# A SwiGLU feed-forward stage whose additions move from GpSimd to VectorE, one per step

## The chip, the core and the metric

The kernel runs on one core of one Trainium2 chip. The metric is the device time of one execution in microseconds. The engines are named as in the profile: PE (TensorE matmuls), DVE (VectorE), ACT (ScalarE), POOL (GpSimd) and SP (SyncE, which here only issues DMAs). A DMA goes to the queue of the engine that issues it; each engine works through its own instructions strictly in order.

## The reference

One block of a streaming encoder: RMSNorm, an input projection, two attention mixers, an output projection with a residual, then the feed-forward part, which is all that the change touches. Everything is float32, S = 2048, D = 1024, D_FF = 2816:

```
h2 = rmsnorm(x, norm2_g)
g = einsum('bsd,df->bsf', h2, w_gate)
u = einsum('bsd,df->bsf', h2, w_up)
x = x + einsum('bsf,fd->bsd', silu(g) * u, w_down)
return rmsnorm(x, normf_g)
```

## The kernel before

**Blocks.** Every product of the feed-forward part is done as a 2x2 product of blocks by a scheme with seven products (P1 to P7) in place of eight; its price is sums of blocks ahead of the products and of results behind them. Each factor is split into a rounded high part (a CAST on ACT, L930) and the rest (a subtraction on DVE, L931), and each product of blocks is three matmuls per 128 rows of the contraction: high by high, high by low, low by high. A step is one of the seven products.

**Stages.** The tokens come in two halves of 1024. In each half there are 11 pairs of a gate and an up matrix, each of a gate's and an up's 14 steps (ORDER: P1, P2, P6, P5, P7, P3, P4) of 12 matmuls (L1054 to L1056); then the Down stage, 7 products of 11 steps of 12 matmuls (L1163 to L1165). Half 0's Down also prepares the other half's h2 blocks (next_h2). In half 0, down_sums makes the four sums of w_down's blocks and writes them to DRAM (wd_d), once for both halves.

**Banks and results.** A matrix has three PSUM banks: A takes P1, P6, P7 and P4, C takes P2, B takes P5 and P3. After P1, P6 and P7, ACT copies A to a tile `u` (L1064); after P7, DVE adds B to it (L1066) and the block (1,1) is done. P3 then accumulates on in B, so its first matmul waits for L1066; P2's and P3's results are added at L1069 and L1072. A gate's block goes through Silu on ACT (L1083), an up's is multiplied with the gate's: block (0,0) on POOL, the other three on DVE (L1087). After the last of the four, `activations` makes the block sums of the result (three on POOL, one on DVE) and POOL's queue writes all seven blocks to DRAM (a_d, L1096).

**What sets the order.** The text of the loop over `steps` (L1257) issues, for step `at`: loads up to 12 steps ahead (6 in Down) on SP, all four sums of a weight matrix when its P1 is 6 steps ahead (L1018 to L1021, POOL), splits 4 steps ahead (3 in Down), the step's matmuls, and what follows from its result. down_sums comes behind the gate's P5: its two loads, four sums on DVE (the same lines L1018 to L1021) and four writes on SP (L1119). `late` holds squares and final scalings of a Down stage, one per step. Weight tiles share 6 buffers (`raw`), split operands 7, and all tiles of [128, 512] float32 (sums, `u`, `t`, x, squares) one pool of 18; a tile's buffer is handed on when its last reader is done.

Of the kernel before, what the change touches and what calls it, by code (L numbers as in the profile page):

```python
# [19 lines left out]
P = 128  # L20
# [39 lines left out]
def block_kernel(  # L60
# [848 lines left out]
    with ExitStack() as c4:  # L909
        def pool(name, bufs):  # L910
            return c4.enter_context(tc.tile_pool(name=name, bufs=bufs, reuse_waits="tile"))

        hop, rawp, opp, t2p, np_ = pool("hop", 1), pool("rawF", 6), pool("opF", 7), pool("t2", 18), pool("nf", 1)
        psF = c4.enter_context(tc.tile_pool(name="psF", bufs=8, space=PSUM, reuse_waits="tile"))
# [7 lines left out]

        def t2(name):
            return t2p.tile([P, 512], F32, name=name, tag="t2")

# [54 lines left out]
        def next_h2(half):  # L980

            for q in range(2):
                cs = slice(q * 256, (q + 1) * 256)
                for k0 in (0, 2):
                    ks_ = slice(k0, k0 + 2)

                    def put(p, src):
                        hi, lo = ops_h[p]
                        split(hi[:, ks_, cs], lo[:, ks_, cs], src)

                    b = {}
# [11 lines left out]
                    nc.gpsimd.tensor_tensor(b12, b22, b12, ALU.subtract)  # L1003
# [5 lines left out]
                    nc.gpsimd.tensor_tensor(b11, b22, b11, ALU.subtract)  # L1009
                    nc.gpsimd.tensor_tensor(b21, b21, b11, ALU.subtract)  # L1010
                    yield
                    put("P6", b11)
                    put("P4", b21)
                    yield

        def sums(a11, a12, a21, a22, eng):
            s = {p: t2(f"s{p}") for p in ("P5", "P6", "P7", "P3")}
            eng(s["P5"], a21, a22, ALU.add)  # L1018
            eng(s["P6"], s["P5"], a11, ALU.subtract)
            eng(s["P7"], a11, a21, ALU.subtract)  # L1020
            eng(s["P3"], a12, s["P6"], ALU.subtract)  # L1021
            return dict(s, P1=a11, P2=a12, P4=a22)

        late = []

        class Matrix:
# [10 lines left out]
            def sum(self):  # L1037
                r = self.r
                self.s = sums(r[0][:, 0], r[0][:, 1], r[1][:, 0], r[1][:, 1], nc.gpsimd.tensor_tensor)

# [37 lines left out]
            def done(self, i, j):  # L1078

                d = self.dst  # L1080
                if not self.up:
                    o = t2("u") if (i, j) == (1, 0) else d[i, j]
# [8 lines left out]
            def activations(self):  # L1091
# [6 lines left out]
                t1, t2_, t4 = t2("t"), t2("t"), t2("t")  # L1098
                sub = nc.gpsimd.tensor_tensor
                put("P1", b11)  # L1100
                put("P3", b22)
                put("P2", b21)
                sub(t1, b12, b11, ALU.subtract)
                sub(b12, b22, b12, ALU.subtract)
                put("P5", t1)
                put("P7", b12)
                sub(t2_, b22, t1, ALU.subtract)
                put("P6", t2_)
                nc.vector.tensor_sub(t4, b21, t2_)
                put("P4", t4)  # L1110

        def down_sums(n):
            r = []
            for f in (n, n + NF // 2):
                r.append(raw([P, 2, 512], "wd"))
                nc.sync.dma_start(out=r[-1].rearrange("p a b -> p (a b)"), in_=w_down[f * P:(f + 1) * P, :])
            s = sums(r[0][:, 0], r[1][:, 0], r[0][:, 1], r[1][:, 1], nc.vector.tensor_tensor)
            for p in ("P5", "P6", "P7", "P3"):
                nc.sync.dma_start(out=wd_d[PLACE[p], n // 2, :, n % 2, :], in_=s[p])  # L1119

        class Down:
# [50 lines left out]
            def square(self, t, i):  # L1172
                sq = t2("sq")
                ss = small.tile([P, 1], F32, name="ssf", bufs=20)
# [13 lines left out]
            def take(self, p):  # L1188
# [17 lines left out]
                elif p == "P4":  # L1206
                    self.add(p, 1, 0)
                    late.extend(partial(self.square, b, 1) for b in q)
                    late.extend(partial(self.finish, b) for b in q)


        steps = []
        for half in range(2):
# [6 lines left out]
            for p in ORDER:  # L1220
                steps += [("down", dn, p, n) for n in range(NF // 2)]
        loads, summed, made = [0], [0], [0]

        def advance_loads(at):
# [32 lines left out]
        for at, s in enumerate(steps):  # L1257
            down = s[0] == "down"
            advance_loads(at)
            advance_sums(at + 6)  # L1260
            advance_splits(at + (3 if down else 4))
            if down:
                s[1].multiply(s[2], s[3])
                if s[2] == "P1" and s[3] < 8:
                    s[1].load_x(s[3])
                if s[1].half == 0:
# [72 lines left out]
```

## Time and profile before

| | |
|---|---|
| median of 3 runs | 2978.04 us (2973.07 to 2979.21) |
| the profiled execution | 2973.52 us, its span 2971.7 us |
| granted TensorE clock, mean | 0.978 of full speed |
| busy in the span | PE 95%, DVE 58%, ACT 46%, POOL 34% |
| the feed-forward part | from about 1562 us of the span to its end |
| half 0: gate and up / Down | 1562 to 2090 / 2090 to 2310 us |
| half 1: gate and up / Down | 2310 to 2750 / 2750 to 2971.7 us |

Times are counted from the span's start. Matmuls overlap in the rows: each is listed with the time from its start to its modelled end, so the pace is read from one start to the next. Behind an instruction, square brackets hold the idle time of its engine before it and what ended that. The clock is the share of full speed granted to TensorE; its two levels are 2.4 and 1.2 GHz. A few matmuls have no record in the trace.

### The profile page before, as it was taken

What the parts mean: (1) busy time and instruction counts of PE and PEld (TensorE: products, weight loads), DVE (VectorE), ACT (ScalarE), POOL (GpSimd) and SP (SyncE); (2) the same over time, 40 slices, a digit from 0 to 9 for tenths busy, and PEclk for the clock granted to TensorE, in tenths of its full rate; (3) what the DMA queues carried; (4) which work ended last, traced back from release to release, by engine and by line L of the source; (5) the groups of instructions that cost most, each with busy time, mean ns of one, the idle gap of its engine ahead of it and who ended that gap; (6) DMA issues with size and microseconds to landing.
All of it is one profiled execution on the core that took longest, in us unless ns stands there. A gap on an engine that the chain in (4) does not pass through costs nothing.

```text
span 2971.7 us, 40975 instructions
## 1 busy us (share of the span) xinstructions
PE 2825.7 (95%) x14538; PEld 2355.2 (79%) x14538; DVE 1715.2 (58%) x3213; ACT 1354.9 (46%) x2752; POOL 1016.4 (34%) x1313
## 2 busy tenths in 40 slices
PE   8999999999999999999997898888999999999997
PEld 7889888789998888777875676777788788888886
DVE  5321411198889888873227656656686655555555
ACT  5211111287788788873334232223455333333443
POOL 3210631134443433331113545534221555554001
PEclk9999999999999999999997999999999999999999
DMA  5342533533532333215444434344767323223764
GB/s 194 125 138 93 150 110 117 181 85 105 145 102 63 97 103 105 82 56 202 163 149 159 145 125 135 118 133 142 252 213 235 122 101 105 103 92 107 259 202 159
DMA packets 160701, 406.75 MB, mean 137 GB/s; under 512 B 24128, under 2 KB 40656, under 8 KB 160496
## 3 DMA queue, kind: packets, MB, share of 16 engines
q1 hardware_dynamic: 121520, 292.31, 31.4%
q0 software_dynamic: 38944, 111.82, 10.6%
q8 instruction: 114, 1.87, 0.3%
q14 instruction: 91, 0.75, 0.1%
q10 hardware_dynamic: 32, 0.01, 0.0%
HBM read 272.35 MB, written 131.66 MB: 136 GB/s over the span
## 4 chain that ended last, share of the span: by engine, by line
PE 73%; DVE 8%; POOL 7%; issue 5%; ACT 4%; DMA 2%; DVEq 0%; POOLq 0%; SPq 0%; ACTq 0%
PE psF L1054 6%; PE psM L255 6%; PE psM L253 6%; PE psM L254 6%; PE psF L1055 6%; PE psF L1056 6%; PE ps L707 6%; PE psS L550 4%; PE psS L551 3%; PE psF L1164 3%; PE psF L1165 3%; PE psF L1163 3%; PE psO L642 3%; DVE wop L931 3%; PE psO L636 2%
## 5 line engine op out<-in xcount | busy, mean ns | idle before, releaser
L1054 PE MATMUL psF<-hhP,wop 128*128 128x512 f32 x1232 | 492.3, 405 | 83.1 <-DVE u L1066 64.4
L1055 PE MATMUL psF<-hlP,wop 128*128 128x512 f32 x1232 | 492.3, 400 | 5.6 <-DVE hlP L931 5.6
L1056 PE MATMUL psF<-hhP,wop 128*128 128x512 f32 x1232 | 490.2, 398 | 1.7 <-DVE wop L931 1.7
L1054 PEld LDWEIGHTS psF<-hhP,wop 128*128 128x128 f32 x1232 | 239.2, 194 | 155.9 <-DVE u L1066 77.8
L580 ACT ACTIVATE p_sb<-p_sb,mx 128x1024 f32<-128x1024 f32 (+7 forms) x384 | 343.8, 902 | 25.1 <-DVE mx L561 17.6
L1055 PEld LDWEIGHTS psF<-hlP,wop 128*128 128x128 f32 x1232 | 239.3, 194 | 53.9 <-DVE hlP L931 6.9
L1056 PEld LDWEIGHTS psF<-hhP,wop 128*128 128x128 f32 x1232 | 238.6, 194 | 53.9 <-DVE wop L931 2.6
L550 PE MATMUL psS<-ks,q 128*128 128x512 f32 (+2 forms) x640 | 271.3, 424 | 3.8 <-DVE mx L567 3.5
L707 PE MATMUL ps<-ident,p_sb 128*128 128x128 f32 x1632 | 251.1, 274 | 9.3 <-ACT thd L733 5.3
L1164 PE MATMUL psF<-dop 128*128 128x512 f32 x616 | 240.2, 390 | 2.7 <-DVE dop L931 2.7
L1163 PE MATMUL psF<-dop 128*128 128x512 f32 x616 | 239.9, 389 | 0.2 <-ACT dop L930 0.2
L1165 PE MATMUL psF<-dop 128*128 128x512 f32 x616 | 239.7, 389 | 0.0
L931 DVE TENSOR_TENSOR wop<-sP,wop 128x512 fp32r<-128x512 f32 x176 | 176.1, 1012 | 98.3 <-ACT wop L930 97.4
L551 PE MATMUL psS<-ks,q 128*128 128x512 f32 (+2 forms) x640 | 232.8, 364 | 0.0
L707 PEld LDWEIGHTS ps<-ident,p_sb 128*128 128x128 f32 x1632 | 194.6, 141 | 40.5 <-ACT thd L733 7.5
L930 ACT CAST wop<-sP 128x512 fp32r<-128x512 f32 x176 | 107.2, 622 | 218.8 <-PE psF L1056 108.5
L253 PE MATMUL psM<-hTh,whi 128*128 128x512 f32 (+1 forms) x528 | 205.7, 391 | 0.5 <-ACT hTh L220 0.5
L254 PE MATMUL psM<-hTl,whi 128*128 128x512 f32 (+1 forms) x528 | 205.5, 390 | 0.6 <-DVE hTl L221 0.5
L255 PE MATMUL psM<-hTh,wlo 128*128 128x512 f32 (+1 forms) x528 | 205.1, 389 | 0.0
L931 DVE TENSOR_TENSOR dop<-wr,dop 128x512 fp32r<-128x512 f32 x154 | 112.4, 730 | 134.4 <-ACT dop L930 134.1
L931 DVE TENSOR_TENSOR wop<-wr,wop 128x512 fp32r<-128x512 f32 x132 | 148.2, 1125 | 64.9 <-ACT wop L930 64.6
L930 ACT CAST dop<-wr 128x512 fp32r<-128x512 f32 x154 | 95.8, 622 | 184.2 <-PE psF L1165 165.9
(210 smaller groups left out, 6338.8 us busy)
## 6 DMA issues: line engine op xcount, KB each, us to landing
ar<-a_d SPq DMA_DIRECT2D x70, 512.0 KB, 3.5
wr<-in_w_gate_dram SPq DMA_DIRECT2D x44, 512.0 KB, 3.9
wr<-in_w_up_dram SPq DMA_DIRECT2D x44, 512.0 KB, 4.4
a_d<-u POOLq DMA_DIRECT2D x88, 256.0 KB, 3.2
wr<-wd_d SPq DMA_DIRECT2D x40, 512.0 KB, 4.4
a_d<-t POOLq DMA_DIRECT2D x66, 256.0 KB, 3.2
q<-fq_d SPq DMA_DIRECT2D x64, 256.0 KB, 3.9
q<-dq_d SPq DMA_DIRECT2D x64, 256.0 KB, 3.9
```

What stands on the lines that cost most here:

```text
L253: nc.tensor.matmul(ps, lh, rh, start=k == 0, stop=False)
L254: nc.tensor.matmul(ps, lh, rl, start=False, stop=False)
L255: nc.tensor.matmul(ps, ll, rh, start=False, stop=k == DK - 1)
L550: nc.tensor.matmul(pm[:, 0:mw], q[:, m, 0, qc], ks[:, m, cols], start=True, stop=False)
L580: nc.scalar.activation(pv, pv, AF.Exp, scale=-1.0, bias=st[m], accum_out=acc)
L707: nc.tensor.transpose(ps[:, (2 * i + s) * P:(2 * i + s + 1) * P], p_of(u, s, m, k0 + i), ident)
L931: nc.vector.tensor_sub(lo, src, f32(hi))
L1054: nc.tensor.matmul(acc, o[:, 0, ks_], hh[:, k, :], start=first and k == 0, stop=False, **go)
L1055: nc.tensor.matmul(acc, o[:, 0, ks_], hl[:, k, :], start=False, stop=False, **go)
L1056: nc.tensor.matmul(acc, o[:, 1, ks_], hh[:, k, :], start=False, stop=k == 3, **go)
L1163: nc.tensor.matmul(acc, a[:, 0, bs], w[:, 0, :], start=first and n == 0, stop=False, **go)
L1164: nc.tensor.matmul(acc, a[:, 0, bs], w[:, 1, :], start=False, stop=False, **go)
```

## The change

All sums of weight blocks (`sums`), the product of block (0,0), the block sums of the result and the subtractions of next_h2 are done by DVE; POOL keeps the DMA issues and the small operations of the final norm. `sums` becomes a generator: one sum is made per call, when the matrix's P1, P2, P6 and P5 come into the window of 7 steps ahead (6 before). down_sums becomes one too: its loads are issued at the gate's P2 and one sum each at P6, P5, P7 and P3, and the writes go out on POOL's queue instead of SP's. `activations` is called twice, after the blocks (0,1) and (1,0). The pool of 18 buffers becomes four rings: `s` (5, sums of gate and up weights), `g` (6, gate blocks), `u` (3, up blocks), `t` (3, sums of the result and of w_down), and one buffer for squares. Loads go out 11 steps ahead instead of 12; Down's x loads start one step later and take the rings' buffers; at the end of Down, squares and final scalings alternate.

```diff
-        hop, rawp, opp, t2p, np_ = pool("hop", 1), pool("rawF", 6), pool("opF", 7), pool("t2", 18), pool("nf", 1)
+        hop, rawp, opp, np_ = pool("hop", 1), pool("rawF", 6), pool("opF", 7), pool("nf", 1)
+        RINGS = dict(s=5, g=6, u=3, t=3)
+        rings = {r: pool(f"ring_{r}", n) for r, n in RINGS.items()}
...
-                    nc.gpsimd.tensor_tensor(b11, b12, b11, ALU.subtract)
+                    nc.vector.tensor_sub(b11, b12, b11)
...
-        def sums(a11, a12, a21, a22, eng):
-            s = {p: t2(f"s{p}") for p in ("P5", "P6", "P7", "P3")}
-            eng(s["P5"], a21, a22, ALU.add)
...
+        def sums(a11, a12, a21, a22, ring):
+            def put(p, a, b, op):
+                o = t2(ring, f"s{p}")
+                nc.vector.tensor_tensor(o, a, b, op)
+                return o
+            s5 = put("P5", a21, a22, ALU.add)
+            yield "P5", s5
+            s6 = put("P6", s5, a11, ALU.subtract)
+            yield "P6", s6
+            yield "P7", put("P7", a11, a21, ALU.subtract)
+            yield "P3", put("P3", a12, s6, ALU.subtract)
...
-                self.s = sums(r[0][:, 0], r[0][:, 1], r[1][:, 0], r[1][:, 1], nc.gpsimd.tensor_tensor)
+                if not hasattr(self, "s"):
+                    r = self.r
+                    b = r[0][:, 0], r[0][:, 1], r[1][:, 0], r[1][:, 1]
+                    self.s, self.rest = dict(P1=b[0], P2=b[1], P4=b[3]), sums(*b, "s")
+                self.s.update([next(self.rest)])
...
-                    d[i] = t2("u")
+                    d[i] = t2("u" if self.up else "g", "u")
...
-                    (nc.gpsimd if (i, j) == (0, 0) else nc.vector).tensor_mul(g, g, d[i, j])
-                    if (i, j) == (1, 0):
-                        self.activations()
+                    nc.vector.tensor_mul(g, g, d[i, j])
+                    if (i, j) in ((0, 1), (1, 0)):
+                        self.activations((i, j) == (1, 0))
...
+                if last:
+                    put("P2", b21)
+                    sub(self.t2, b21, self.t2)
+                    put("P4", self.t2)
+                    return
+                t1, self.t2 = t2("t", "t"), t2("t", "t")
                 put("P1", b11)
+                sub(t1, b12, b11)
+                put("P5", t1)
+                sub(self.t2, b22, t1)
+                sub(b12, b22, b12)
+                put("P7", b12)
                 put("P3", b22)
+                put("P6", self.t2)
...
-            s = sums(r[0][:, 0], r[1][:, 0], r[0][:, 1], r[1][:, 1], nc.vector.tensor_tensor)
-            for p in ("P5", "P6", "P7", "P3"):
-                nc.sync.dma_start(out=wd_d[PLACE[p], n // 2, :, n % 2, :], in_=s[p])
+            yield
+            for p, o in sums(r[0][:, 0], r[1][:, 0], r[0][:, 1], r[1][:, 1], "t"):
+                nc.gpsimd.dma_start(out=wd_d[PLACE[p], n // 2, :, n % 2, :], in_=o)
+                yield
...
-                    self.xs[t, i] = t2("x1")
+                    self.xs[t, i] = t2("ggtttuuusssssggg"[2 * t + i], "x1")
...
-                if loads[0] >= at + (12 if s[0] == "in" else 6):
+                if loads[0] >= at + (11 if s[0] == "in" else 6):
...
-                if s[0] == "in" and s[2] == "P1":
+                if s[0] == "in" and s[2] in SUM_AT:
                     s[1].sum()
...
-            advance_sums(at + 6)
+            advance_sums(at + 7)
...
-                if s[1].half == 0 and not s[1].up and s[2] == "P5":
-                    down_sums(s[1].n)
+                if s[1].half == 0 and not s[1].up:
+                    if s[2] == "P2":
+                        wd = down_sums(s[1].n)
+                    if s[2] != "P1":
+                        next(wd, None)
```

In the order that follows, the number at a row's start is its place on the engine; `wd` is a tile of w_down, `wr` one of a gate's or up's weights, `psF` a PSUM bank, `wop` a split operand, and the numbers behind names tell tiles apart. DVE before, in half 0, from the gate's P2 add (L1069) to behind its P7 add (L1066):

```order
2366 L1069 TENSOR_TENSOR u_18452<-psF_18457,u_18452 128x512
2367 L931 TENSOR_TENSOR wop_18552<-wr_18350,wop_18552 128x512
2368 L1018 TENSOR_TENSOR sP5_18521<-wd_18517,wd_18519 128x512
2369 L1019 TENSOR_TENSOR sP6_18522<-sP5_18521,wd_18517 128x512
2370 L1020 TENSOR_TENSOR sP7_18523<-wd_18517 128x512
2371 L1021 TENSOR_TENSOR sP3_18524<-wd_18519,sP6_18522 128x512
2372 L931 TENSOR_TENSOR wop_18569<-sP6_18473,wop_18569 128x512
2373 L931 TENSOR_TENSOR wop_18586<-sP5_18472,wop_18586 128x512
2374 L1066 TENSOR_TENSOR u_18548<-psF_18504,u_18548 128x512
```

DVE after the change at the same place (P2 add L1081, P7 add L1078; L934 is the split, L1023 a sum, L1113 the last block sum of the result):

```order
2434 L934 TENSOR_TENSOR wop_18531<-wr_18369,wop_18531 128x512
2435 L1081 TENSOR_TENSOR u_18456<-psF_18463,u_18456 128x512
2436 L1113 TENSOR_TENSOR t_18412<-u_18292,t_18412 128x512
2437 L934 TENSOR_TENSOR wop_18553<-wr_18369,wop_18553 128x512
2438 L1023 TENSOR_TENSOR sP7_18550<-wd_18478 128x512
2439 L1023 TENSOR_TENSOR sP5_18608<-wr_18526 128x512
2440 L934 TENSOR_TENSOR wop_18573<-sP6_18482,wop_18573 128x512
2441 L1023 TENSOR_TENSOR sP3_18570<-wd_18480,sP6_18522 128x512
2442 L1023 TENSOR_TENSOR sP6_18628<-sP5_18608,wr_18525 128x512
2443 L934 TENSOR_TENSOR wop_18590<-sP5_18458,wop_18590 128x512
2444 L1023 TENSOR_TENSOR sP7_18647<-wr_18525,wr_18526 128x512
2445 L1078 TENSOR_TENSOR u_18546<-psF_18509,u_18546 128x512
```

The four sums of w_down no longer stand in one piece ahead of the gate's P7 add: two of them, with the last block sum of the result, stand behind the P2 add, each with a split or a sum of the next matrix's weights beside it, and three sums of that matrix (sP5, sP6, sP7 from `wr`) have come in from POOL.

POOL before, behind the products of a pair of half 0 (DMAs L1096 write the result's blocks, L1104 and L1107 are block sums, the rest sums of weights):

```order
816 L1096 DMA a_d_99<-u_18287 128x512
817 L1096 DMA a_d_99<-t_18422 128x512
818 L1096 DMA a_d_99<-u_18198 128x512
819 L1107 TENSOR_TENSOR t_18423<-u_18251,t_18422 128x512
820 L1096 DMA a_d_99<-t_18423 128x512
821 L1096 DMA a_d_99<-t_18424 128x512
822 L1018 TENSOR_TENSOR sP5_18472<-wr_18351 128x512
823 L1019 TENSOR_TENSOR sP6_18473<-sP5_18472,wr_18350 128x512
824 L1020 TENSOR_TENSOR sP7_18474<-wr_18350,wr_18351 128x512
```

POOL after, the same place (L1108 writes the result's blocks, L1134 w_down's sums):

```order
773 L1108 DMA a_d_99<-t_18411 128x512
774 L1108 DMA a_d_99<-u_18292 128x512
775 L1108 DMA a_d_99<-t_18412 128x512
776 L1108 DMA a_d_99<-u_18203 128x512
777 L1134 DMA wd_d_100<-sP5_18501 128x512
778 L1134 DMA wd_d_100<-sP6_18522 128x512
779 L1108 DMA a_d_99<-t_18412 128x512
780 L1134 DMA wd_d_100<-sP7_18550 128x512
781 L1134 DMA wd_d_100<-sP3_18570 128x512
```

POOL's arithmetic is gone from its queue, and the four writes of w_down's sums, which stood on SP, stand between the writes of the result.

ACT before, at the start of the feed-forward part (L880 belongs to the stage ahead; L930 casts of the first matrix's weights and of h2's first blocks):

```order
1281 L880 ACTIVATE h2b_16813<-psT_16821,gcol_80 128x256
1282 L930 CAST hhP1_16860<-h2r_16886 128x4x256
1283 L930 CAST hhP1_16860<-h2r_16887 128x4x256
1284 L930 CAST wop_16938<-sP6_16879 128x512
1285 L930 CAST wop_16941<-sP5_16878 128x512
1286 L930 CAST wop_16959<-sP7_16880 128x512
```

ACT after:

```order
1281 L933 CAST wop_16922<-wr_16879 128x512
1282 L933 CAST wop_16947<-sP6_16889 128x512
1283 L933 CAST wop_16950<-sP5_16887 128x512
1284 L933 CAST wop_16970<-sP7_16891 128x512
1285 L933 CAST wop_16998<-sP3_16893 128x512
1286 L933 CAST wop_17026<-wr_16880 128x512
1287 L933 CAST hhP1_16869<-h2r_16895 128x4x256
```

The casts of five weight operands that stood behind the first casts of h2 (hhP1) stand ahead of them.

## Rows read from the trace of the kernel before

**Rows 1.** Windows: stretch, length, busy us (instructions) by engine, TensorE clock, DMA share, GB/s.

```profile
1562.00:1654.00 92.00, 68.49 (x241) 51.77 (x242) 66.59 (x62) 34.28 (x50) 38.49 (x29) 0.82 0.46 151
1654.00:2075.20 421.20, 367.17 (x1520) 295.56 (x1519) 251.89 (x257) 126.08 (x218) 201.13 (x170) 0.93 0.40 132
...
2089.90:2309.90 220.00, 217.04 (x949) 177.36 (x948) 161.32 (x222) 111.87 (x209) 46.86 (x41) 1.00 0.70 238
2309.90:2340.00 30.10, 23.60 (x92) 18.82 (x91) 20.59 (x23) 10.68 (x23) 18.50 (x20) 0.89 0.33 110
2340.00:2750.00 410.00, 406.09 (x1773) 329.34 (x1772) 220.52 (x254) 145.91 (x253) 213.22 (x191) 1.00 0.29 102
```

**Rows 2.** Timeline of PE: start us, us, engine, line, operation [idle before <- releaser].

```profile
1700.82 0.80 PE L1054 MATMUL psF<-hhP,wop 128*128 128x512 f32 x1 [5.94 <-DVE u L1066]
...
1706.05 0.40 PE L1054 MATMUL psF<-hhP,wop 128*128 128x512 f32 x1
...
1719.20 0.39 PE L1056 MATMUL psF<-hhP,wop 128*128 128x512 f32 x1
...
1721.24 0.39 PE L1056 MATMUL psF<-hhP,wop 128*128 128x512 f32 x1
```

**Rows 3.** Windows, one pair of half 0.

```profile
1700.80:1747.60 46.80, 40.90 (x168) 33.00 (x168) 27.71 (x29) 13.90 (x24) 22.68 (x20) 0.94 0.38 128
```

**Rows 4.** Waits of PE, 1654 to 2090: us in total, times, longest.

```profile
PE psF L1054 <- DVE u L1066: 54.0, 10, 6.9
```

**Rows 5.** Timeline of DVE, a gate (to 1700) and an up matrix.

```profile
1693.39 1.78 DVE L1020 TENSOR_TENSOR sP<-wd 128x512 f32<-128x512 f32 x1
...
1700.09 0.68 DVE L1066 TENSOR_TENSOR u<-psF,u 128x512 f32<-128x512 f32 x1
...
1721.61 0.69 DVE L1066 TENSOR_TENSOR u<-psF,u 128x512 f32<-128x512 f32 x1 [1.94 <-ACT u L1064]
1722.22 0.68 DVE L931 TENSOR_TENSOR wop<-sP,wop 128x512 fp32r<-128x512 f32 x1
...
1734.05 0.68 DVE L1069 TENSOR_TENSOR u<-psF,u 128x512 f32<-128x512 f32 x1
```

**Rows 6.** Timeline of POOL, the same stretch.

```profile
1699.58 1.71 POOL L1021 TENSOR_TENSOR sP<-wr,sP 128x512 f32<-128x512 f32 x1
...
1733.71 0.56 POOL L1096 DMA_DIRECT2D a_d<-t  x1 [0.30 <-POOL t L1107]
```

**Rows 7.** Waits of PE, half 1 (2345 to 2750).

```profile
PE psF L1054 <- DVE u L1066: 3.9, 10, 0.4
```

**Rows 8.** DMA issues, 1654 to 2075.2: operation, count, KB each, median us to landing.

```profile
wd_d<-sP SPq DMA_DIRECT2D x39, 256.0 KB, 5.5
a_d<-u POOLq DMA_DIRECT2D x36, 256.0 KB, 3.1
...
wr<-in_w_gate_dram SPq DMA_DIRECT2D x16, 512.0 KB, 6.8
```

**Rows 9.** DMA issues of half 1 (2345 to 2747).

```profile
wr<-in_w_gate_dram SPq DMA_DIRECT2D x16, 512.0 KB, 3.6
```

**Rows 10.** Waits of PE, 1562 to 1654.

```profile
PE psF L1054 <- ACT hhP L930: 14.0, 4, 8.6
...
PE psF L1054 <- ACT u L1064: 3.9, 2, 3.2
```

**Rows 11.** Timeline, start of the FFN: POOL and PE.

```profile
1567.15 1.72 POOL L1021 TENSOR_TENSOR sP<-wr,sP 128x512 f32<-128x512 f32 x1
...
1579.04 0.80 PE L1054 MATMUL psF<-hhP,wop 128*128 128x512 f32 x1 [8.59 <-ACT hhP L930]
```

**Rows 12.** Timeline of PE, turn into half 1.

```profile
2331.89 0.79 PE L1054 MATMUL psF<-hhP,wop 128*128 128x512 f32 x1 [6.50 <-DVE u L1066]
```

**Rows 13.** Waits of PE in Down (2090 to 2320).

```profile
PE psF L1164 <- DVE dop L931: 2.7, 5, 1.5
```

More of the change, by code (lines that the diff above doesn't have):

```diff
@@ L921, in raw, with t2 @@
             return rawp.tile(shape, F32, name=name, tag="raw")
-        def t2(name):
-            return t2p.tile([P, 512], F32, name=name, tag="t2")
+        def t2(ring, name):
+            return rings[ring].tile([P, 512], F32, name=name, tag=ring)
         def bank():
@@ L1001, in next_h2 @@
                     yield
-                    nc.gpsimd.tensor_tensor(b11, b12, b11, ALU.subtract)
-                    nc.gpsimd.tensor_tensor(b12, b22, b12, ALU.subtract)
+                    nc.vector.tensor_sub(b11, b12, b11)
+                    nc.vector.tensor_sub(b12, b22, b12)
                     put("P3", b22)
@@ L1008, in next_h2 @@
                     yield
-                    nc.gpsimd.tensor_tensor(b11, b22, b11, ALU.subtract)
-                    nc.gpsimd.tensor_tensor(b21, b21, b11, ALU.subtract)
+                    nc.vector.tensor_sub(b11, b22, b11)
+                    nc.vector.tensor_sub(b21, b21, b11)
                     yield
@@ L1014, in next_h2 @@
                     yield
-        def sums(a11, a12, a21, a22, eng):
-            s = {p: t2(f"s{p}") for p in ("P5", "P6", "P7", "P3")}
-            eng(s["P5"], a21, a22, ALU.add)
[L1019 to L1022, printed above, removed]
+        def sums(a11, a12, a21, a22, ring):
[9 more added lines that the diff above has]
+            yield "P3", put("P3", a12, s6, ALU.subtract)
         late = []
@@ L1037, in sum @@
             def sum(self):
-                r = self.r
-                self.s = sums(r[0][:, 0], r[0][:, 1], r[1][:, 0], r[1][:, 1], nc.gpsimd.tensor_tensor)
+                if not hasattr(self, "s"):
[3 more added lines that the diff above has]
+                self.s.update([next(self.rest)])
             def split(self, p):
@@ L1081, in done @@
                 if not self.up:
-                    o = t2("u") if (i, j) == (1, 0) else d[i, j]
+                    o = t2("g", "u") if (i, j) == (1, 0) else d[i, j]
                     nc.scalar.activation(o, d[i, j], AF.Silu)
@@ L1086, in done, with activations @@
                     g = self.gate.dst[i, j]
-                    (nc.gpsimd if (i, j) == (0, 0) else nc.vector).tensor_mul(g, g, d[i, j])
-                    if (i, j) == (1, 0):
-                        self.activations()
-            def activations(self):
+                    nc.vector.tensor_mul(g, g, d[i, j])
+                    if (i, j) in ((0, 1), (1, 0)):
+                        self.activations((i, j) == (1, 0))
+            def activations(self, last):
                 g, half, n = self.gate.dst, self.half, self.n
@@ L1096, in put @@
                     nc.gpsimd.dma_start(out=a_d[half, PLACE[p], n // 2, :, n % 2, :], in_=src)
-                t1, t2_, t4 = t2("t"), t2("t"), t2("t")
-                sub = nc.gpsimd.tensor_tensor
-                put("P1", b11)
-                put("P3", b22)
[L1102 to L1110, printed above, removed]
+                sub = nc.vector.tensor_sub
+                if last:
[4 more added lines that the diff above has]
+                t1, self.t2 = t2("t", "t"), t2("t", "t")
+                put("P1", b11)
+                sub(t1, b12, b11)
[3 more added lines that the diff above has]
+                put("P7", b12)
+                put("P3", b22)
+                put("P6", self.t2)
         def down_sums(n):
@@ L1172, in square @@
             def square(self, t, i):
-                sq = t2("sq")
+                sq = np_.tile([P, 512], F32, name="sq")
                 ss = small.tile([P, 1], F32, name="ssf", bufs=20)
@@ L1207, in take @@
                     self.add(p, 1, 0)
-                    late.extend(partial(self.square, b, 1) for b in q)
-                    late.extend(partial(self.finish, b) for b in q)
+                    for b in q:
+                        late.extend((partial(self.square, b, 1), partial(self.finish, b)))
         steps = []
@@ L1222, in block_kernel @@
         loads, summed, made = [0], [0], [0]
+        SUM_AT = ("P1", "P2", "P6", "P5")
         def advance_loads(at):
@@ L1263, in block_kernel @@
                 s[1].multiply(s[2], s[3])
-                if s[2] == "P1" and s[3] < 8:
-                    s[1].load_x(s[3])
+                if s[2] == "P1" and 0 < s[3] < 9:
+                    s[1].load_x(s[3] - 1)
                 if s[1].half == 0:
```

## The prediction

> **What bounds the kernel now.** I read the busy table by stages first [rows 1]: only the FFN changes, so what matters is how far TensorE (PE) is from its own pace there. That pace comes from two rows of the PE timeline nine matmuls apart: 1719.20 to 1721.24, 0.2267 us each [rows 2]. A step of the FFN's gate and up part is 12 matmuls, 2.72 us; a pair (a gate and an up matrix, 14 steps) 168, 38.09 us. In half 0 a pair takes 46.80 us at a mean granted clock of 0.94 [rows 3]: 8.7 us are lost in each. By the same reckoning the stretch 1654 to 2075.2 holds 1520 recorded matmuls, 344.6 us, in 421.2 us: 76.6 lost. The stretch 2340 to 2750, the same work in half 1, holds 1773 in 410.0 at clock 1.00 and 220.5 us of DVE, against 251.9 in half 0 [rows 1].
>
> The waits of PE say where: 54.0 us in 10 waits are the first matmul of P3 waiting for DVE's L1066, the add of the P7 block [rows 4]. P3 accumulates into the PSUM bank that L1066 reads. One of them on the PE timeline: the matmul at 1700.82 follows 5.94 us of idle, and the next twelve, 1700.82 to 1706.05, take 5.23 us instead of 2.72: TensorE has fallen to its lower level, 1.2 GHz (0.44 us per matmul), after the idle [rows 2]. 5.94 + 2.5 is the 8.7 of a pair, but for a few tenths.
>
> The DVE timeline says why [rows 5]. Ahead of L1066 stand, in program order, four sums of w_down blocks (the third, at 1693.39, 1.78 us) and two splits; L1066 itself starts at 1700.09 and takes 0.68. In the same microseconds POOL runs its sums of weight blocks up to 1701.29 [rows 6]. Where POOL rests, DVE's instructions start 0.61 us apart (1721.61, 1722.22) and take 0.68 to 0.69: L1066 there starts as soon as ACT's copy is there, and PE doesn't stop. So the sums cost twice: they stand in the queue, and both engines run them at about a third of DVE's own pace. L1066, with one input in PSUM, keeps 0.68 even beside POOL's L1021.
>
> **The change, part by part.**
>
> *All sums and products on DVE, spread.* In a pair of half 0 POOL gives up 12 operations (8 sums, 1 product, 3 subtractions); by the order DVE has 28 instructions in a pair now and 40 then. At 0.61 us that is 24.4 us of the pair's 38.1, so DVE has room, if no POOL arithmetic runs beside it, and none is left there but DMA issues. Now the place that matters: between the up's P3 add and the gate's L1078 (the new number of L1066) stand the same four w_down sums, and three of the next matrix's, between splits. I count from the end of the up's P7 (0), by PE's steps and 0.61 us per DVE instruction: the P3 add starts at 4.5; product, subtractions, the first two w_down sums and splits bring DVE to 11.1, where it does the gate's P2 add; then the P4 subtraction at 11.7, sP7 of w_down at 12.9, the next matrix's sP5 at 13.5, and the rest by about 17.5. L1078 is wanted at 19.7 (19.05 for the seven steps and 0.6 for ACT's copy). PE then has seven matmuls, 1.59 us, of P7's successors to run before P3, which the copy and L1078 use up. With 1.5 to 2 us to spare the 5.94 us idle goes, and the slow twelve matmuls with it. Gain: 76.6, less up to 4 matmuls without a record (0.9), less 2 for small waits that stay: 74. The last number is the size of half 1's remainder, 3.9 over ten waits [rows 7].
>
> *What may be late next.* Three things in this queue wait for transfers. sP5 of the next matrix needs its second weight half, whose buffer is free only after the gate's P4 split at 9.9; in half 0 the w_gate loads took 6.8 in the median, but the SP queue there holds the w_down writes too, 5.5 each, which go [rows 8]; if it lands in 3.6, as in half 1 [rows 9], the wait is nothing. sP7 and sP3 of w_down write into a ring of three buffers: they need the writes of sP5 and of the P4 subtraction to have landed; a write on POOL's queue took 3.1, issue included, so 12.5 and about 15.7, just in time or 0.6 late [rows 8].
>
> *Writes of w_down sums on POOL's queue instead of SP's.* 4 more issues a pair, 11 in all. An issue took 0.56 on POOL at 1733.71 with DVE's L1069 beside it at 0.68 [rows 5, 6]: 6 us of POOL in 38. I cost it at nothing; what covers it is that nothing else is on POOL. With the cover gone it is the second rival.
>
> The Trainium skill, in "SBUF — State Buffer", "SBUF: two separate sides", warns of a trap: for a DMA issued by GpSimd that core writes the descriptors through the port pair it shares with VectorE, and an operation in a two-port mode locks it out until it ends; "Who interferes with whom" there adds, as inferred, that a tensor_tensor takes only the read side. By the first alone the 11 writes would be late behind a DVE busy two thirds of the time, and the sum would be rival 2's; by the second it stands. The rows agree with the second for one tensor_tensor with an input in PSUM (0.56 at 1733.71); a long run of them with both inputs in SBUF no row shows.
>
> *Start of the FFN* (1562 to 1654). 241 matmuls, 54.6 us, take 92.0: 37.4 lost [rows 1]. PE waits 14.0 for ACT's h2 casts (8.59 before 1579.04) and 3.9 for the P7 copies [rows 10, 11]. The late load of P2's second half hangs on a weight buffer that POOL's L1021 holds until 1568.87 [rows 11]. Four sums at DVE's pace are over by about 1564, but now casts and sums precede the first h2 cast, so P1 starts some 2 us later than now while P2's second half comes at about 1575.3 against 1579.04: 3.7 gained. The 3.2 wait for the first P7 copy (the longest of its row) falls with POOL's sums, and 2.5 of slow matmuls behind it. Total 9.4, taken as 9; bounds: 5 lost (if the late P1 only shifts everything) and 20 gained (more than half of the 37.4).
>
> *Turn into half 1* (2309.9 to 2340). PE waits 6.50 for L1066 and then runs slow: 6.5 + 2.5 = 9 [rows 12]. DVE had the final scaling and splits stretched beside POOL's sums there. They end: 8 gained, bounds 5 and 9.
>
> *Half 1.* 3.9 in all stands behind the same add [rows 7]; with POOL quiet I take the whole, 4 rounded; bounds −4 (ten more such waits, DVE being fuller) and 4.
>
> *Down.* next_h2's 16 subtractions come to DVE: 16 × 0.61 = 9.8 us of a stage of 220.0 in which DVE is busy 161.3 [rows 1]. Splits that waited 2.7 in all [rows 13] lose the POOL neighbour and get more queue: 2 gained, bounds −5 and 2.7. Rings (17 buffers and one for squares against 18), loads one step later (11 against 12) and the x loads from the rings cost nothing where loads land 3 to 7 us after issue and stand ten steps (27 us) ahead.
>
> Sum: 74 + 9 + 8 + 4 + 2 = 97. The profiled execution took 2973.5 us (span 2971.7); 2876.5 is left. The median before is 4.5 above the profiled run, so I put the time at 2880, allowing nothing else.
>
> **The rivals.**
>
> *1. The weight load or the writes hold up DVE's queue, a little.* Speaking for it: the slack of 1.5 to 2 us and the 6.8 of w_gate [rows 8]. A load landing at 9.9 + 6.8 = 16.7 puts L1078 1.2 late; 10 gates cost 12 us, or up to 37 with the 2.5 of slow matmuls at each: 2892 to 2917. Against: in half 1, without w_down writes on SP, the same loads landed in 3.6 [rows 9].
>
> *2. The writes on POOL come back late.* Place: sP3 of w_down waits for the P4 write, issued at 12.3; what follows needs 1.8 us before 19.7, so from 5.6 us of landing on each further microsecond idles PE. At 10 us: 4.4 + 2.5 = 6.9 per gate, 10 × (8.7 − 6.9) + 23 (the four other terms) = 41 gained: 2937. Slower than before only if a gate loses over 8.7 + 2.3 = 11, that is from 14.1 us of landing on; at 18 us 14.9 per gate, 10 × 6.2 − 23 = 39 lost: 3017. Against: no landing median of the stage exceeds 6.8 [rows 8]. The Trainium skill's trap, cited above from "SBUF — State Buffer", would act at this place.
>
> *3. The change doesn't free DVE*: what stretched its sums was not POOL. Then 40 instructions at the 1.7 of its sums [rows 5] would be 68 us a pair against 46.8: slower by 200 and more. From 1.17 us an instruction on it would lose. Against: 0.61 apart wherever POOL rests.
>
> **How the numbers follow.** My forecast, 2862 to 2892, has 0.62; below it (more back at the start and in Down) 0.04; rival 1 0.16; rival 2 on its near side, 2917 to 2970, 0.09; no change, within 0.2% or 6 us (what a measurement here can tell from none), 0.03; rival 2 on its far side 0.05; rival 3 0.01. Range 2860 to 2918: the forecast and rival 1 and the edges on either side, 0.8. Faster 0.91, same 0.03, slower 0.06.
>
> **What would show it.** Right: in the new profile the half-0 pair takes 38 to 39 us at clock 1.00; PE's waits for L1078 between 1654 and the Down stage sum to under 5 us; DVE's sums and splits take 0.69 and no POOL arithmetic but the small sums of squares runs in the FFN; the gap at the turn is gone. Wrong: waits of DVE for DMAs ahead of w_down's sP7 or sP3 (rival 2) or of the next matrix's sP5 (rival 1), with PE idle at each gate's P3; or DVE instructions of over 1 us with POOL at rest (rival 3). My forecast falls if PE still idles over 2 us at the gates.

## The result and the profile after

The changed kernel takes 2874.64 us (median of 4, 2870.43 to 2877.16) against 2976.38 on the same chip: ratio 0.9657, interval 0.9640 to 0.9674. The forecast was 2880. The profiled execution took 2874.22 us (span 2872.4, clock 0.993), 99.3 us of span less than before.

The first row is the windows view of 360 us in the gate and up stage of half 0 (columns as in [rows 1]), the second one of 380 us in half 1:

```profile
1630.00:1990.00 360.00, 352.08 (x1531) 285.72 (x1530) 236.16 (x366) 127.64 (x219) 55.15 (x102) 1.00 0.47 157
2250.00:2630.00 380.00, 378.87 (x1661) 308.70 (x1660) 231.09 (x353) 137.56 (x237) 37.87 (x70) 1.00 0.32 106
```

In half 0 360 us now hold 1531 matmuls, 0.235 us each; before, 421.2 us held 1520, 0.277 each [rows 1]. The clock is 1.00. DVE issues 366 instructions in 236.16 us, 0.65 each, where 257 took 251.89, 0.98 each. What PE and DVE wait for in the same stretch:

```profile
PE psF L1066 <- DVE u L1078: 7.9, 7, 1.9
```

```profile
DVE sP L1023 <- DMA wd_d<-sP: 13.0, 9, 2.1
DVE sP L1023 <- DMA a_d<-t: 12.2, 10, 2.0
...
DVE t L1113 <- DMA a_d<-t: 2.0, 2, 1.5
```

Against 54.0 in [rows 4], 7.9 us are left, at seven gates (6.0 at six from 1654 to the Down stage, the stretch of [rows 4]), and DVE's own waits name the cause: buffers of ring `t`, to be written by the next sum, whose last writes to DRAM have not landed. One such gate on DVE's timeline, behind the P7 add of the up matrix ahead of it:

```profile
1697.83 0.69 DVE L1078 TENSOR_TENSOR u<-psF,u 128x512 f32<-128x512 f32 x1 [1.21 <-ACT u L1076]
...
1708.45 0.68 DVE L1081 TENSOR_TENSOR u<-psF,u 128x512 f32<-128x512 f32 x1
1709.05 0.68 DVE L1113 TENSOR_TENSOR t<-u,t 128x512 f32<-128x512 f32 x1
1709.65 0.68 DVE L934 TENSOR_TENSOR wop<-wr,wop 128x512 fp32r<-128x512 f32 x1
1712.41 0.69 DVE L1023 TENSOR_TENSOR sP<-wd 128x512 f32<-128x512 f32 x1 [2.07 <-DMA wd_d<-sP]
...
1715.57 0.69 DVE L1023 TENSOR_TENSOR sP<-wd,sP 128x512 f32<-128x512 f32 x1 [1.26 <-DMA a_d<-t]
...
1718.11 0.68 DVE L1078 TENSOR_TENSOR u<-psF,u 128x512 f32<-128x512 f32 x1
```

the issues of the two writes that it waits for, on POOL's timeline:

```profile
1707.02 0.54 POOL L1134 DMA_DIRECT2D wd_d<-sP  x1
...
1710.03 0.54 POOL L1108 DMA_DIRECT2D a_d<-t  x1 [1.26 <-DVE t L1113]
```

and the end of it on PE's: an idle of 0.86 us, after which PE goes on at its full pace, where 5.94 were followed by twelve slow matmuls [rows 2].

```profile
1718.85 0.50 PE L1066 MATMUL psF<-hhP,wop 128*128 128x512 f32 x1 [0.86 <-DVE u L1078]
1719.18 0.40 PE L1067 MATMUL psF<-hlP,wop 128*128 128x512 f32 x1
1719.42 0.39 PE L1068 MATMUL psF<-hhP,wop 128*128 128x512 f32 x1
```

The landings (columns as in [rows 8]):

```profile
wd_d<-sP POOLq DMA_DIRECT2D x38, 256.0 KB, 5.1
...
wr<-in_w_gate_dram SPq DMA_DIRECT2D x16, 512.0 KB, 4.3
a_d<-t POOLq DMA_DIRECT2D x28, 256.0 KB, 2.8
```

The last median hides what matters: of the result's writes from `t`, the one that the gate waits for is the last block sum's, and there it let DVE go on 5.5 us after its issue (1710.03 to 1715.57). The DMA engines are nearly full in these microseconds, 0.98 by the windows view (columns as in [rows 1]):

```profile
1708.00:1712.00 4.00, 4.00 (x19) 3.32 (x18) 2.34 (x4) 2.32 (x4) 1.08 (x2) 1.00 0.98 335
```

By the starts of the P7 add (L1066, L1078) on DVE, the gain falls to these stretches:

| stretch, by the P7 adds | before | after | gain |
|---|---|---|---|
| ahead of the FFN (last matmul of the stage before) | 1551.80 | 1550.19 | 1.6 |
| from there to the 2nd (first up) | 80.2 | 68.5 | 11.7 |
| 2nd to 22nd: half 0 | 458.7 | 393.6 | 65.2 |
| 22nd to 24th: Down and turn | 262.2 | 250.1 | 12.1 |
| 24th to 44th: half 1 | 389.1 | 384.7 | 4.4 |
| 44th to the end: Down and end | 229.8 | 225.4 | 4.3 |

### The profile page after: what moved, and what is told of

Its sections match the earlier page's. It is cut to its first block, busy times and chain, and to the rows that moved or that the text cites. A ratio compares the mean times of both kernels' runs of the same rounds, so it can differ in the third digit from the quotient of the medians.

```text
span 2872.4 us, 40841 instructions
## 1 busy us (share of the span) xinstructions
PE 2794.5 (97%) x14538; PEld 2337.8 (81%) x14538; DVE 1705.9 (59%) x3493; ACT 1356.6 (47%) x2752; POOL 608.4 (21%) x1077
## 4 chain that ended last, share of the span: by engine, by line
PE 70%; issue 19%; POOL 4%; ACT 3%; DVE 2%; DMA 1%; POOLq 0%; DVEq 0%; SPq 0%; ACTq 0%
PE psM L253 6%; PE psM L255 6%; PE psM L254 6%; PE ps L707 6%; PE psF L1180 4%; PE psF L1181 4%; PE psF L1179 4%; PE psS L550 4%; PE psS L551 4%; PE psO L642 3%; PE psF L1066 3%; PE psF L1068 3%; PE psF L1067 3%; PE psO L636 2%; PE psO L635 2%
## 5 line engine op out<-in xcount | busy, mean ns | idle before, releaser
L1066 PE MATMUL psF<-hhP,wop 128*128 128x512 f32 x1232 | 480.2, 395 | 25.1 <-ACT hhP L933 12.4
L1067 PE MATMUL psF<-hlP,wop 128*128 128x512 f32 x1232 | 482.8, 392 | 3.5 <-DVE hlP L934 3.4
L1068 PE MATMUL psF<-hhP,wop 128*128 128x512 f32 x1232 | 482.0, 392 | 1.5 <-DVE wop L934 1.5
L580 ACT ACTIVATE p_sb<-p_sb,mx 128x1024 f32<-128x1024 f32 (+7 forms) x384 | 343.6, 901 | 25.1 <-DVE mx L561 17.7
L1066 PEld LDWEIGHTS psF<-hhP,wop 128*128 128x128 f32 x1232 | 232.4, 189 | 92.6 <-DVE u L1078 22.3
L1068 PEld LDWEIGHTS psF<-hhP,wop 128*128 128x128 f32 x1232 | 232.9, 189 | 51.1 <-DVE wop L934 1.9
L1067 PEld LDWEIGHTS psF<-hlP,wop 128*128 128x128 f32 x1232 | 233.0, 189 | 50.3 <-DVE hlP L934 5.0
L934 DVE TENSOR_TENSOR dop<-wr,dop 128x512 fp32r<-128x512 f32 x154 | 106.3, 690 | 136.2 <-ACT dop L933 135.9
L1076 ACT COPY u<-psF 128x512 f32<-128x512 f32 x132 | 77.5, 587 | 201.0 <-PE psF L1068 201.0
L934 DVE TENSOR_TENSOR wop<-sP,wop 128x512 fp32r<-128x512 f32 x176 | 120.8, 688 | 76.4 <-ACT wop L933 76.1
```

The lines of the kernel that those rows point to most:

```text
L1066: nc.tensor.matmul(acc, o[:, 0, ks_], hh[:, k, :], start=first and k == 0, stop=False, **go)
L1067: nc.tensor.matmul(acc, o[:, 0, ks_], hl[:, k, :], start=False, stop=False, **go)
L1068: nc.tensor.matmul(acc, o[:, 1, ks_], hh[:, k, :], start=False, stop=k == 3, **go)
```

## The experiments

Each is timed against the kernel before on its chip; the ratio stands behind the median.

| run | weight sums | w_down's sums on DVE | median us | ratio (interval) |
|---|---|---|---|---|
| b_spread | POOL | spread | 2950.78 | 0.992 (0.990 to 0.994) |
| b_products_dve | POOL | one piece | 2936.95 | 0.987 (0.985 to 0.989) |
| b_sums_dve | DVE, four at once | one piece | 2879.79 | 0.968 (0.967 to 0.970) |
| a_pool_run | POOL, four at once | spread | 2887.73 | 0.970 (0.968 to 0.971) |
| a_sums_pool | POOL, one per step | spread | 2874.43 | 0.967 (0.965 to 0.968) |
| a_pool_one_piece | POOL, one per step | one piece | 2865.49 | 0.962 (0.960 to 0.964) |
| after2 (the new kernel) | DVE, one per step | spread | 2875.90 | 0.966 (0.964 to 0.967) |
| wd_on_sp | DVE, one per step | spread | 2873.60 | 0.966 (0.964 to 0.967) |
| ring5 | DVE, one per step | spread | 2860.14 | 0.961 (0.960 to 0.963) |
| one_piece | DVE, one per step | one piece | 2860.32 | 0.961 (0.960 to 0.962) |

**ring5: five buffers for the ring that waits.**

```diff
-        RINGS = dict(s=5, g=6, u=3, t=3)
+        RINGS = dict(s=4, g=6, u=2, t=5)
-  t2("ggtttuuusssssggg"[2 * t + i], "x1")
+  t2("ggtttttuussssggg"[2 * t + i], "x1")
```

> The new kernel with other ring sizes: s 4, g 6, u 2, t 5 instead of 5, 6, 3, 3 (the sum stays 17). Theory: what is left of the gates' stalls in half 0 (6.0 us of waits for L1078 after 1650, seven of ten gates about 1.2 us longer than the rest) comes from DVE waiting for writes to land before it may reuse a t buffer; with five there is no such wait, and the time falls by 7 to 10 us against the new kernel, to 2865 to 2868. Rival: DVE is simply too full ahead of the P7 add, and the waits for the writes only fill time that it would lose anyway; then the time stays within 3 us.

15.8 us below the new kernel on the same chip (after2), more than expected, and with one_piece the fastest version of all. In the stretch 1630 to 1990 PE waits for nothing and is busy throughout:

```profile
1630.00:1990.00 360.00, 360.00 (x1580) 293.27 (x1579) 239.91 (x372) 132.70 (x228) 55.13 (x102) 1.00 0.48 165
```

w_down's writes land no sooner (6.2 in the median), but DVE doesn't wait for one of them, and for the result's only twice, 2.4 us in all. The P7 adds stand 19.16 us apart from matrix to matrix, where one takes 19.04 at PE's pace. Of the 15.8 the same marks give 12.3 in half 0 (382.4 from the 2nd to the 22nd against 394.7 in after2). So DVE was not too full; what was left at the gates was the wait for the landings.

**after2 and wd_on_sp: the same again, and the writes on SP.**

```diff
-                nc.gpsimd.dma_start(out=wd_d[...], in_=o)
+                nc.sync.dma_start(out=wd_d[...], in_=o)
```

> The new kernel once more, unchanged, to be compared with the others on one chip: 2870 to 2878 by either theory. Theory on the tail: the 4.4 us by which its last stretch (last matmul to the end) was shorter than before is not of the change and comes or goes from execution to execution; rival: it stays at 11.5 us.

> The new kernel with the writes of w_down's sums on SP's queue again. Theory: which queue carries them matters little; SP now waits for each sum before it issues the next load, so loads come a little later: 2872 to 2890. Rival (late writes on POOL): the residual waits are of POOL's queue; with SP they go and the time is 2864 to 2868.

2875.9 and 2873.6: the queue makes no difference to the total. DVE still waits for wd_d writes, 11.0 us in 8 waits between 1640 and 1990. At the gates it does make one. The waits of PE between 1630 and 2010, of after2 and of wd_on_sp:

```profile
PE psF L1066 <- DVE u L1078: 8.9, 9, 2.6
```

```profile
PE psF L1066 <- DVE u L1078: 5.6, 2, 3.1
```

w_down's writes land in 4.1 in the median on SP's queue, 5.0 on POOL's (1630 to 1990), and half 0 is 5.4 shorter; 4.4 more at the end of the span take that back (last section). So the rival that laid the waits to POOL's queue was right on most of the gates and wrong on the time.

**one_piece: the spreading undone, on ring5.**

```diff
-                    if s[2] == "P2":
-                        wd = down_sums(s[1].n)
-                    if s[2] != "P1":
-                        next(wd, None)
+                    if s[2] == "P5":
+                        for _ in down_sums(s[1].n):
+                            pass
```

> The ring sizes of ring5, and the four sums of w_down in one piece behind the gate's P5, as in the kernel before; POOL still does no arithmetic. Theory (neighbour): POOL's arithmetic beside DVE was the cause, four sums at 0.61 us are 2.4 us and fit ahead of the P7 add; 2865 to 2880. Rival (queue): the piece in the queue was the cause; half or more of the old stall returns at each gate, 4 to 8 us, and the time is 2910 to 2950.

2860.3, the same as ring5. With POOL quiet, the place and the piece cost nothing.

**b_sums_dve: half of the move, nothing else, on the kernel before.**

```diff
-   self.s = sums(..., nc.gpsimd.tensor_tensor)
+   self.s = sums(..., nc.vector.tensor_tensor)
```

> The kernel before with one edit: the four sums of each gate or up matrix's blocks are done by DVE instead of POOL, all four in one piece where they stood; w_down's sums stay in one piece, products and block sums of the result stay where they were. Theory (neighbour): with POOL's sums gone, DVE is at 0.69 us in that stretch, and although eight sums now stand ahead of the gate's P7 add (11 instructions, 6.7 us, in about 8.6 us) the stall goes: 2885 to 2905. Rival (queue): more in one piece ahead of the add makes the stall longer: 2970 or more.

One word gives 94 of the 102 us; in half 0 alone it gives more than the whole change (386.3 from the 2nd to the 22nd P7 add, 393.6 in the new kernel). Eight sums now stand ahead of the gate's P7 add, and still it is in time but for a few tenths (2.4 us in 7 waits of PE between 1680 and 1990). DVE there:

```profile
1751.29 0.68 DVE L1018 TENSOR_TENSOR sP<-wd 128x512 f32<-128x512 f32 x1
1751.89 0.68 DVE L931 TENSOR_TENSOR wop<-wr,wop 128x512 fp32r<-128x512 f32 x1
1752.50 0.68 DVE L1019 TENSOR_TENSOR sP<-sP,wd 128x512 f32<-128x512 f32 x1
1753.10 0.68 DVE L1020 TENSOR_TENSOR sP<-wd 128x512 f32<-128x512 f32 x1
1753.70 0.68 DVE L1021 TENSOR_TENSOR sP<-wd,sP 128x512 f32<-128x512 f32 x1
```

The sum that took 1.78 at 1693.39 in [rows 5] takes 0.68, in the same piece at the same place. The queue theory is refuted.

**b_spread and b_products_dve: the other two parts alone, on the kernel before.** The first makes down_sums a generator like the new one, its writes on SP; the second is

```diff
-   (nc.gpsimd if (i, j) == (0, 0) else nc.vector).tensor_mul(g, g, d[i, j])
+   nc.vector.tensor_mul(g, g, d[i, j])
-                sub = nc.gpsimd.tensor_tensor
+                sub = nc.vector.tensor_tensor
```

> The kernel before with one edit: the four sums of w_down are spread, one behind each of the gate's P6, P5, P7 and P3 with its write on SP, loads at P2; POOL keeps all its arithmetic. Theory (neighbour): two sums instead of four stand ahead of the P7 add, but these and the splits are still stretched to 1.7 us beside POOL; about 2.5 of the 5.9 us of stall stay, and the time is 2915 to 2945. Rival (queue): the stall goes, and the time is 2885 to 2905.

> The kernel before with the other half of POOL's arithmetic moved: the product of block (0,0) and the block sums of the result are done by DVE, the sums of gate and up weights stay on POOL as they were, w_down's sums in one piece on DVE. Theory: the eight weight sums still stand in one run behind POOL's writes of the result, beside DVE's piece; the run starts some 3 us earlier in each pair, since POOL's own block sums ahead of it go; so a part of the stall goes: 2930 to 2965. Rival (any relief of POOL's queue does it): 2880 to 2900.

Spreading gives 23 us, less than expected; the products give 38, as expected. In both, PE still waits about 4 us at a gate. POOL in b_products_dve, behind its last write of the result:

```profile
1725.95 0.54 POOL L1096 DMA_DIRECT2D a_d<-t  x1 [0.66 <-DVE t L1109]
1726.50 1.30 POOL L1018 TENSOR_TENSOR sP<-wr 128x512 f32<-128x512 f32 x1
...
1737.50 1.71 POOL L1021 TENSOR_TENSOR sP<-wr,sP 128x512 f32<-128x512 f32 x1
```

and DVE beside it, from the first sum of w_down to the P7 add:

```profile
1730.60 0.72 DVE L1018 TENSOR_TENSOR sP<-wd 128x512 f32<-128x512 f32 x1 [2.24 <-DMA wd<-in_w_down_dram]
...
1739.68 0.68 DVE L1066 TENSOR_TENSOR u<-psF,u 128x512 f32<-128x512 f32 x1
```

POOL's eight sums run without a break from 1726.50 to 1739.21, up to the P7 add, because in POOL's order they stand behind writes that wait for the up's last products. Not all of this stall is POOL's: DVE also waits 2.24 us for a load of w_down ahead of its sums (15.8 in 7 waits between 1654 and 2075), which it doesn't in the kernel before.

**a_sums_pool, a_pool_run, a_pool_one_piece: the weight sums back on POOL.** In `sums`, with a_pool_run also taking all four at P1, 6 steps ahead (rings s 6, g 6, u 2, t 3), and a_pool_one_piece having ring5's rings and one_piece's edit:

```diff
-                nc.vector.tensor_tensor(o, a, b, op)
+                (nc.gpsimd if ring == "s" else nc.vector).tensor_tensor(o, a, b, op)
```

> The new kernel with the sums of gate and up weights on POOL again, one per step as now; w_down's sums, the products and the rest stay on DVE. Theory (neighbour): DVE has 32 instead of 40 instructions in a pair, but those beside POOL's sums take 1.7 instead of 0.69, and POOL's writes stand behind its sums: stalls at the gates return in part, 2895 to 2945. Rival (queue): fewer instructions on DVE, so 2865 to 2876.

> The new kernel with the sums of gate and up weights on POOL, all four of a matrix in one piece 6 steps ahead, as in the kernel before (rings s 6, g 6, u 2, t 3); w_down's sums stay spread on DVE, products and block sums on DVE. Theory after the earlier runs (a run of POOL sums beside DVE costs, single ones are absorbed in DVE's spare time): DVE instructions at 1.7 us come in runs again ahead of the gate's P7 add, and the time is 2890 to 2945. Rival (it is the number of POOL's sums and not their order): as with one POOL sum per step, 2872 to 2879.

> The ring sizes of ring5; POOL does the sums of gate and up weights, one per step; w_down's four sums in one piece on DVE behind the gate's P5. Theory: only the one or two POOL sums that fall beside the piece stretch it, by a microsecond or two, and DVE has that to spare: 2860 to 2880. Rival (the piece ahead of the add costs as soon as POOL works at all): 2900 to 2950.

The first was a miss for my theory: 2874.4, no slower than the new kernel, with eight POOL sums in every pair. That is a sum of two differences: counted from the last matmul of the stage before, its 2nd P7 add comes 10.3 us later than the new kernel's, and from there to the 22nd it is 7.5 shorter (386.1 against 393.6). Its DVE and POOL at a gate:

```profile
1718.76 0.69 DVE L1023 TENSOR_TENSOR sP<-wd 128x512 f32<-128x512 f32 x1 [1.43 <-DMA wd_d<-sP]
1719.01 1.59 POOL L1023 TENSOR_TENSOR sP<-wr 128x512 f32<-128x512 f32 x1 [1.45 <-ACT wop L933]
1719.37 1.78 DVE L934 TENSOR_TENSOR wop<-sP,wop 128x512 fp32r<-128x512 f32 x1
...
1723.05 0.68 DVE L934 TENSOR_TENSOR wop<-sP,wop 128x512 fp32r<-128x512 f32 x1
```

A single POOL sum still stretches the DVE instruction beside it from 0.68 to 1.78, but the next ones run free, and a microsecond here or there is within what DVE has to spare. What costs in half 0 is a run of eight, as before the change and in b_products_dve. Whether a run of four costs is not shown: a_pool_run was meant to bring it, but in half 0 its POOL sums come one or two at a time, waiting for buffers between, and a DVE instruction takes 0.72 us on average there, against 0.70 in a_sums_pool (1640 to 2000). It is some 11 us slower than the new kernel by the ratios (2887.7, below the range that I gave), but its 2nd P7 add alone comes 11.3 us later; from there on the two take the same time. With one POOL sum per step even the piece is harmless at the gates (381.7 from the 2nd to the 22nd add, 382.4 in ring5; 2865.5 in all).

**idle_sums_pool and echo_sums_pool: needless POOL work beside ring5's DVE.** At each weight sum, respectively:

```diff
+   nc.gpsimd.tensor_tensor(np_.tile([P, 512], F32, name="sq"), normfb[:, 0:512], normfb[:, 512:1024], ALU.add)
```

```diff
+   nc.gpsimd.tensor_tensor(np_.tile([P, 512], F32, name="sq"), o, o, ALU.add)
```

> The kernel of ring5, and POOL does one needless addition of two 128x512 tiles in SBUF (the halves of normfb, the result unused) at each sum of a gate or up matrix, 8 in a pair; DVE's instructions are unchanged. Theory (neighbour): the additions alone bring the stretched DVE instructions (some 8 in a pair from 0.69 to 1.7) and stalls back: 2885 to 2960. Rival (queue): no change against ring5 beyond 3 us.

> The kernel of ring5, and POOL doubles each sum of a gate or up matrix into a spare tile (one input tile read twice, result unused), so that its needless work now keeps pace with the sums, 8 in a pair and never in a run. Theory: 2860 to 2880, with some DVE instructions beside POOL's at over 1 us and no stall at the gates. Rival (any POOL arithmetic brings the stalls back): 2900 or more.

The first took 3022.32, ratio 1.016 (1.0145 to 1.0176), outside both forecasts, and it isn't the run that I meant: its additions wait for nothing, so POOL did them at once instead of one per sum, 77 in a row, and its first write of a w_down sum came behind them:

```profile
1562.13 137.16 POOL L1052 TENSOR_TENSOR sq<-normfb 128x512 f32<-128x512 f32 x77
1699.24 0.57 POOL L1135 DMA_DIRECT2D wd_d<-sP  x1
```

That shows the neighbour's effect on DVE's pace by itself. DVE, with ring5's order, at the start of the FFN and, POOL done with additions, in the steady part:

```profile
1563.89 1.74 DVE L1023 TENSOR_TENSOR sP<-sP,wr 128x512 f32<-128x512 f32 x1
1565.56 1.75 DVE L1023 TENSOR_TENSOR sP<-wr 128x512 f32<-128x512 f32 x1
1567.23 1.75 DVE L1023 TENSOR_TENSOR sP<-wr,sP 128x512 f32<-128x512 f32 x1
...
1749.39 0.68 DVE L1023 TENSOR_TENSOR sP<-sP,wd 128x512 f32<-128x512 f32 x1
1749.99 0.68 DVE L1082 TENSOR_TENSOR u<-psF,u 128x512 f32<-128x512 f32 x1
```

1.67 us from start to start beside POOL, 0.60 without it. The 3rd P7 add comes 84 us after ring5's (1720.31 against 1635.96); from there its matrices are 19.15 apart, like ring5's, until POOL has a run of additions again at the turn: from the 22nd to the 25th add 344.7 us against 267.9. These 84 and 77 are all of the 162 us, but they are not the slow pace alone. In each, DVE has one long wait for a write that stands behind the additions in POOL's queue, and PE idles 23.7 and 40.1 us at these two:

```profile
1701.65 1.34 DVE L1121 TENSOR_TENSOR t<-u,t 128x512 f32<-128x512 f32 x1 [17.70 <-DMA wd_d<-sP]
...
2421.37 0.69 DVE L1114 TENSOR_TENSOR t<-u,t 128x512 f32<-128x512 f32 x1 [45.80 <-DMA a_d<-t]
```

So the run shows what POOL's additions do to DVE's instructions, not what that costs the kernel; for the cost b_sums_dve stands. The echo, one per sum, took 2884.21 (0.968, 0.967 to 0.969), 4 us over my range; its steady gates are 19.1 to 20.0 apart with no stall worth the name, but its 2nd P7 add comes 7.8 us later than ring5's, counted from the last matmul of the stage before, and its Down and turn take 238.0 from the 22nd to the 23rd add, against 229.8 in ring5. The cause of these two stays open.

## Why the prediction was right, step by step

*The cause.* Right, and now shown: POOL's sums stretch DVE's (idle_sums_pool, rows), and without the stretch DVE isn't late (b_sums_dve, one_piece). The prediction said that the sums cost twice, by their place in the queue and by the neighbour. The first half fails: the place costs nothing once POOL is quiet (one_piece equals ring5; b_sums_dve has more in the queue and no stall), and little while it isn't (b_spread, 23 us). "If no POOL arithmetic runs beside it" was too strict too: in half 0 single POOL sums are absorbed (a_sums_pool, a_pool_one_piece); a run of eight is what DVE couldn't bear. At the start of the FFN the two are 10.3 and 4.5 us later at the 2nd P7 add than the new kernel and ring5, so there POOL's sums cost something even so.

The rows agree with the Trainium skill, "SBUF — State Buffer", "Who interferes with whom": a VectorE instruction with two SBUF inputs contends with a GpSimd instruction that reads SBUF, and one with a single SBUF input, outside the two-port modes, doesn't. L1066 with its PSUM input kept 0.68 beside POOL [rows 5, 6].

*Half 0.* 74 forecast, 65.2 measured between the 2nd and the 22nd add. The step that failed is the landing: the prediction took 3.1 us for a write on POOL's queue, from the writes of the result, though 5.5 stood in the line above for w_down's own writes on SP's [rows 8]. w_down's writes landed in 5.1, and so late did the result's last: at the gate shown DVE went on 5.4 us after the issue of the one (1707.02 to 1712.41) and 5.5 after that of the other. By the prediction's own reckoning, counted from the end of the up's P7 (1697.17, 0.66 ahead of its L1078), L1081 would start at 11.1, sP7 of w_down at 12.9 and sP3 at about 15.7 at the latest; they started at 11.3, 15.2 and 18.4. So the order of events was right and one duration too short, by which the 1.5 to 2 us to spare were gone. Rival 1 names the writes in its heading, but its price is the weight load's, which DVE hardly waited for (1.5 us in 2 waits between 1620 and 2005). ring5 gives the missing part back. Two signs of being right were missed by a little: a pair takes 39.4 us (38 to 39 was named), and PE's waits for L1078 from 1654 on are 6.0 (under 5).

*Rival 2*, writes that come back late: its sign came true, DVE waiting for DMAs ahead of w_down's sP7 and sP3 with PE idle at seven gates, its price didn't. POOL issued each write in 0.54 beside a DVE busy 236 of 360 us, w_down's landed 6.5 us after issue at the most, and with these writes on SP (wd_on_sp) the time is the same. What of the 5 us is POOL's queue and what the full DMA engines no run parts. Of the Trainium skill's two statements weighed there ("SBUF — State Buffer", "SBUF: two separate sides", and the exception for tensor_tensor), the trace agrees with the exception: beside DVE's tensor_tensors, now most of them with both inputs in SBUF, the result's writes from `t` landed in 2.8 in the median.

*Rival 3* is out: 0.65 us an instruction.

*Start of the FFN*: 9 forecast, 11.7 measured to the 2nd add. Counted from the last matmul of the stage before, the first matmul comes at 15.3 instead of 10.3 and P2's second half at 24.1 instead of 27.2: 3.1 earlier, 3.7 forecast. With the weight sums back on POOL (a_sums_pool) 10.3 us of this stretch are lost again, so most of its gain goes with them.

```profile
1565.44 0.79 PE L1066 MATMUL psF<-hhP,wop 128*128 128x512 f32 x1 [7.69 <-ACT hhP L933]
...
1574.27 0.50 PE L1066 MATMUL psF<-hhP,wop 128*128 128x512 f32 x1 [2.14 <-ACT hhP L933]
```

*Turn and Down*: 8 and 2 forecast, 12.1 together. *Half 1*: 4 and 4.4. The last stretch was forecast at nothing and gave 4.3, all behind the last matmul (below); 1.6 us of the span's gain lie ahead of the FFN, which the change doesn't touch. So 97 against 99 is partly luck: 9 too much in half 0, 11 too little elsewhere.

## What to carry to other kernels

Before splitting work between two vector engines, look at what the rows of each cost while the other is at work: work given to the idle engine can slow the busy one by more than it takes off it, most of all where an in-order queue bunches it into a run. Ahead of a wait on the bounding engine count the instructions by their pace beside their neighbours, and move the neighbour before moving the order. Needless or early work on an engine that also issues writes holds these up, and with them whoever needs their buffers (17.7 and 45.8 us in idle_sums_pool). In a small ring written out by DMA, count each buffer's life to the landing of that very write, not of a similar one.

## What was not expected of the hardware

The time from the last matmul's start to the end of the span is 15.8 to 15.9 us in the five kernels that write w_down's sums on SP's queue (before, b_sums_dve, b_spread, b_products_dve, wd_on_sp) and 11.5 to 11.8 in the nine that write them on POOL's. My expectation, that it comes and goes, was wrong, and wd_on_sp differs from after2 in that queue alone. The output DMAs are issued in the same rhythm in both (8 in 6.63 and 6.62 us), and no transfer runs in the last microseconds. What stands there is POOL's closing DRAIN, the end of its instructions, which takes 9.40 us in the five and 4.33 to 4.34 in the nine. In the source view (ns of the shortest, median and longest; the longest is the one), wd_on_sp and after2:

```profile
L1355 POOLq DRAIN  x3: 40/93/9397, 2859.2 to 2869.1; - x3
```

```profile
L1355 POOLq DRAIN  x3: 40/102/4334, 2869.3 to 2874.9; - x3
```

Why it is longer the traces don't show, so that stays open. In wd_on_sp the 4.4 us at the end stand against a half 0 that is 5.4 shorter (389.3 from the 2nd to the 22nd add, 394.7 in after2), so the totals are close.

None of the seven idles of PE left in half 0 (0.86 us the one shown, 1.9 the longest) took its clock down: it is 1.00 over the stretch, where a pair before had 0.94 [rows 3].
